# Two-layer hybrid block on one core: triangular substitutions of two groups moved from VectorE to GpSimd, fills re-ordered

## The chip, the cores and the metric

The kernel runs on one core of a Trainium2 chip. The metric is the device time of one execution in microseconds (us), as the median of several runs.

## What is computed

Two layers of a diffusion backbone over 512 latent tokens and 256 context tokens of width 1024. In each layer one projection of the normalised input feeds three token mixers, which are gated, projected and merged:

```python
h = rms_norm(x, norm_g) * (1.0 + scale) + shift
za, ga, zb, gb, zc, gc, zg = jnp.split(h @ w_in, list(IN_CUTS), axis=-1)
ya, yac = rwkv7_branch(za, zac, ...)
yb = dense_block_attention(qb_, jnp.concatenate([kbc, kb_], axis=1), ...)
yc = window_attention(qc_, kc_, vc_, kcc, vcc, c_sink)
x_new = x + gate * merge_branches((ya, yb, yc), (ga, gb, gc), zg, w_branch_out, w_out)
```

The change sits in the first mixer, a recurrence over tokens in both directions, with one 64x64 state S for each of 8 heads:

```python
def step(S, inp):
    r_t, w_t, k_t, v_t, kk_t, a_t = inp
    sa = jnp.einsum('bhvk,bhk->bhv', S, kk_t)
    S = (S * w_t[:, :, None, :] - sa[..., None] * (kk_t * a_t)[:, :, None, :]
         + v_t[..., None] * k_t[:, :, None, :])
    return S, jnp.einsum('bhvk,bhk->bhv', S, r_t)
```

## The kernel before

**The recurrence in chunks.** The 768 tokens are cut into 12 chunks of 64 (`NCH`), and the scan over tokens becomes a scan over chunks. Within a chunk the update needs the inverse of a 64x64 unit triangular matrix for each head and direction. `rwkv_inverse` makes the inverses of a group of four chunks at once (`NS` = 4, `NG` = 3 groups a layer). It loads the matrices (`TT`, four DMAs, L641 and L642), transposes 32x32 blocks on VectorE (L647), cuts out a triangle on GpSimd (`affine_select`, L651), and inverts the 32x32 diagonal blocks by substitution: 30 values of j, each with a multiply (L657) and an add (L659) on VectorE, of j·(31−j) elements per partition, each reading what the one before wrote. Then two transposes on VectorE (L662, L663), and matmuls for the off-diagonal blocks on TensorE: `zp`, then `yp`, in two halves (n0). GpSimd clears a part of the result (L684).

**A chunk's step.** `rwkv_step` is a chain through PE and the engines that empty PSUM: `Rp` (state times input), `Up` (inverse times Rp), `Sp` and `Yp` (new state, output). `rwkv_scores` prepares the products of the chunk two ahead (`scps`, masked on VectorE at L623 and L625). So every `Rp` on PE in the trace is the start of one step. The inverse of the next group is made meanwhile, by a generator `ahead`, which is advanced once behind each of the first three steps of a group; its matmuls come in the group's fourth step (i % NS == NS − 1). The fourth step cannot be passed without them, since `in_line()` keeps PE's instructions in the order in which the code emits them.

**Fills.** Between the pieces of the chain PE works on other projections (`tiles`, `proj`, `gemm_steps`), which have no part in the recurrence. `pace(n)` emits n units of them. In layer 0 a unit is a quarter of the 24 matmuls (12 of 512 columns, 12 of 256) that use one loaded piece of weights; in layer 1 it is 3 matmuls. A piece of weights is loaded as `wf` (L162), copied by ScalarE to a rounded part `wh` (L165), and GpSimd makes the rest `wl` (L166); `wf`, `wh` and `wl` have four buffers each. The table `FILL` gives for each layer: units ahead of the recurrence, units at its first inverse, units at each yield of that inverse's matmuls, units at the three pieces of a step (and of a group's fourth step), units at the last readout. What is left of the fills runs at the end of the layer's attention, with nothing between.

**What sets the order.** A list scheduler orders each engine's instructions by priority bands: `band(b)`, lower first, and SERVE = −1 (weights and what empties PSUM for the fills) ahead of all. With B = 10·layer, scores and steps are in B + 1, the fills of the first inverse in B + 4. Every engine and SyncE's DMA queue then run in that fixed order, each instruction waiting for its inputs and its buffer.

Of the kernel before, what the change touches and what calls it, by code (L numbers as in the profile page):

```python
# [14 lines left out]
ALU = mybir.AluOpType  # L15
# [4 lines left out]
P = 128  # L20
# [9 lines left out]
GB, RB, CB = 2, 3, 2  # L30


FILL = ((48, 36, 2, (2, 2, 2), (3, 3, 3), 2), (72, 56, 4, (2, 2, 2), (3, 3, 3), 2))

QUEUES = (("scalar", "sync", "sync", "scalar"), ("sync", "scalar", "sync", "sync"))

# [1 line left out]
NS, NG = 4, 3  # L38
# [22 lines left out]
def build(tc, A, out):  # L61
    nc = tc.nc
    V, S, G, TE, DMA = nc.vector, nc.scalar, nc.gpsimd, nc.tensor, nc.sync
# [11 lines left out]
    @contextmanager  # L75
    def band(b):

        keep, mine = tc.cur_priority, bands.get(b, b * 1000000)
        tc.cur_priority = mine
        yield  # L80
        bands[b] = tc.cur_priority
        tc.cur_priority = keep
# [64 lines left out]
    @contextmanager  # L147
    def in_line():
        line["on"] = True
        yield  # L150
        line["on"] = False

    def mm(o, l, r, start=True, stop=True, **kw):
        queued(TE.matmul(o, l, r, start=start, stop=stop, **kw))  # L154
# [336 lines left out]
    def rwkv(l, D, last, DL, B, pace, zlast):  # L491

        with tc.tile_pool(name="rw", bufs=1, reuse_waits="tile") as rp:
            yo = rp.tile([P, 4, T], F32, name="yo")
            st = {"seen": set(), "S": None}
            parts, YB = {}, {}

            def scores(i):
                if i < NCH:
                    parts[i] = yield from rwkv_scores(l, last, rp, i)  # L500

            def invert(g):
                if g < NG:
                    YB[g] = rp.tile([P, 32, 64], F32, tag="YB", name="YB", bufs=2)
                    yield from rwkv_inverse(l, rp, g, YB[g])

            def rest(*gens):
                for g in gens:
                    for _ in g:
                        pass  # L510

            with band(B + 1):
                rest(scores(0), scores(1))
                ahead = invert(0)
                for _ in range(3):
                    next(ahead)
            with band(B + 4), tc.issue_after(zlast):
                pace(FILL[l][1])
            with band(B + 1), in_line():
                for _ in ahead:  # L520
                    pace(FILL[l][2])
                ahead = out = iter(())
                for i in range(NCH):
                    if i % NS == 0:
                        rest(ahead)
                        ahead = invert(i // NS + 1)
                    nxt = scores(i + 2)
                    step = rwkv_step(l, last, i, yo, st, DL, rp, parts.pop(i), YB[i // NS])
                    for n in FILL[l][3 if i % NS < NS - 1 else 4]:
                        next(step, None)  # L530
                        next(nxt, None)
                        if i % NS == NS - 1:
                            next(ahead, None)
                        next(out, None)
                        pace(n)
                    rest(step, nxt)
                    if i % NS < NS - 1:
                        next(ahead, None)
                    if i in READY and (i > 3 or not last):
                        rest(out)  # L540
                        out = readout(l, D, rp, yo, READY[i])
                for _ in out:
                    pace(FILL[l][5])

# [90 lines left out]
    def rwkv_inverse(l, rp, g, YB):  # L635

        TT = rp.tile([P, 8, NS, 64], F32, tag="TT", name="TT")
        cs = slice(g * NS, (g + 1) * NS)
        for b0 in (0, 64):

            DMA.dma_start(TT[b0:b0 + 32], tt_d[l][b0:b0 + 32, :, cs])  # L641
            DMA.dma_start(TT[b0 + 32:b0 + 64, :, :, 0:32], tt_d[l][b0 + 32:b0 + 64, :, cs, 32:64])  # L642
        inv = rp.tile([P, 1536], F32, tag="inv", name="inv")
        MB, tmp = inv[:, 0:1024], inv[:, 1024:1536]
        YK = YB[:, :, 32:64]
        TT4 = TT.rearrange("p c s t -> p (c s) t")
        V.transpose(MB, TT4[:, :, 0:32].rearrange("p n j -> p j n"))  # L647

        M3 = MB.rearrange("p (j i) -> p i j", i=32)
        Y3 = YK.rearrange("p j i -> p i j")  # L650
        G.affine_select(YK, MB.rearrange("p (j i) -> p j i", i=32),  # L651
                        [[1, 32], [-1, 32]], ALU.is_gt, 0.0, base=0, channel_multiplier=0)
        V.memset(YB.rearrange("p n c -> p (n c)")[:, 32:2048:65], 1.0)
        for j in range(30, 0, -1):
            n = 31 - j
            t3 = tmp[:, 256 * (j % 2):256 * (j % 2) + j * n].rearrange("p (i c) -> p i c", c=n)
            V.tensor_tensor(t3, M3[:, 0:j, j:j + 1].to_broadcast([P, j, n]),  # L657
                            Y3[:, j:j + 1, j + 1:32].to_broadcast([P, j, n]), ALU.mult)
            V.tensor_tensor(Y3[:, 0:j, j + 1:32], Y3[:, 0:j, j + 1:32], t3, ALU.add)  # L659
            if j in (22, 12):  # L660
                yield
        V.transpose(YB[:, :, 0:32].rearrange("p n j -> p j n"), YK)  # L662
        V.transpose(MB.rearrange("p (n j) -> p n j", j=32), YB[:, :, 0:32])  # L663
        for b0 in (32, 96):
            S.copy(YB[b0:b0 + 32, :, 32:64], YB[b0:b0 + 32, :, 0:32])
        X13 = MB.rearrange("p (n j) -> p n j", j=32)
        yield
        for n0 in range(0, 32, 16):
            zp = rps.tile([P, 16, 32], F32, tag="r", name="zp", bufs=RB)
            for n in range(16):  # L670
                for b0 in (0, 64):
                    mm(zp[b0 + 32:b0 + 64, n, :], TT4[b0:b0 + 32, n0 + n, 32:64], X13[b0:b0 + 32, n0 + n, :])
            z3 = tmp.rearrange("p (n j) -> p n j", j=32)
            for b0 in (32, 96):
                S.copy(z3[b0:b0 + 32], zp[b0:b0 + 32])
            yield
            yp = rps.tile([P, 16, 32], F32, tag="r", name="yp", bufs=RB)
            for n in range(16):
                for b0 in (0, 64):
                    mm(yp[b0:b0 + 32, n, :], z3[b0 + 32:b0 + 64, n, :], YB[b0 + 32:b0 + 64, n0 + n, 32:64])  # L680
            S.copy(YB[0:32, n0:n0 + 16, 32:64], yp[0:32])
            V.tensor_copy(YB[64:96, n0:n0 + 16, 32:64], yp[64:96])
        for b0 in (32, 96):
            G.memset(YB[b0:b0 + 32, :, 0:32], 0.0)  # L684
# [731 lines left out]
    for l in range(2):  # L1416
        last = l == 1
# [3 lines left out]
        B = 10 * l  # L1421
# [22 lines left out]
        def tiles():  # L1444

            zb = [(T_CQ + j, zb_d[l][j], (LAT,) if last and j < 2 else BOTH, "raw") for j in range(4)]
            zc = [(T_ZC + j, zb_d[l][4 + j], (LAT,) if last and j < 4 else BOTH, "raw") for j in range(6)]
            ga, gb, gc = ([(t + j, g_d[l][4 * n + j], segs, "silu") for j in range(4)]
                          for n, t in enumerate((T_GA, T_GB, T_GC)))
            todo = zb[2:] + zc[4:] + zc[:4] + zb[:2] + ga + gb if last else zb + ga + gb + zc  # L1450
            todo += gc + [(T_ZG + j, th_zg[l][j], segs, "tanh") for j in range(24)]
            for a in todo:
                yield from proj(l, hh, hl, *a, side)
                yield

        steps = tiles()

        def pace(n):

            for _ in zip(range(n), steps):  # L1460
                pass
# [3 lines left out]
        with band(B + 4):  # L1465
            pace(FILL[l][0])
        ss = cpool.tile([P, 6, 10], F32, tag="ss", name="ss")
        if last:
            cctx.close()
            with band(B + 3):  # L1470
                gqa_tokens(l, F, last, ss)
        rwkv(l, D, last, DL, B, pace, zlast)
        weights["queue"] = getattr(nc, QUEUES[l][2])
        with band(B + 4), tc.issue_after(line["last"]):
            pace(22 * 8 - sum(FILL[l][0:2]) - 2 * FILL[l][2] - NG * (3 * sum(FILL[l][3]) + sum(FILL[l][4])) - 4 * FILL[l][5])

# [162 lines left out]
```

## Time and profile before

| | |
|---|---|
| median of 3 runs | 2433.22 us (2431.24 to 2439.78) |
| profiled execution, time / span | 2433.78 / 2432.1 us |
| mean granted TensorE clock | 0.947 |
| PE busy | 2166.8 us (89%) |
| DVE (VectorE) busy | 1278.8 us (53%) |
| ACT (ScalarE) busy | 894.1 us (37%) |
| POOL (GpSimd) busy | 844.3 us (35%) |

Shares are averages over stages with different limits. The recurrence of layer 0 runs from about 360 to 660 us of the span, that of layer 1 from about 1690 to 1920 us. A timeline row gives start, duration, engine, line, operation, what it writes and reads, shape and count; in brackets the idle time ahead of it and what ended that.

### The profile page before, as it was taken

Reading aid. Unit: us, or ns where it says so; the run is one execution under the profiler, and the core shown is the slowest. Engines: PE = TensorE matmul, PEld = TensorE weight load, DVE = VectorE, ACT = ScalarE, POOL = GpSimd, SP = SyncE. Lnnn points to the kernel's source line nnn. Section 1 sums busy time; section 2 is a strip of 40 time slices with the busy share of each in tenths; the row PEclk is TensorE's granted clock in tenths of the full one; section 3 lists DMA queues with packets and bytes.
Section 4 is the critical chain, followed back from the end, with each engine's and each line's share of the span. In section 5 each row is a group of like instructions: output and inputs, shape, how many; then the busy total and the mean of one; then the engine's idle time right before and its main releaser. Section 6 shows DMA issues by size and latency. Waiting matters only on the chain. (4 is left out here: it accounts for less than half of the span.)

```text
span 2432.1 us, 42833 instructions
## 1 busy us (share of the span) xinstructions
PE 2166.8 (89%) x16824; PEld 1657.7 (68%) x16824; DVE 1278.8 (53%) x2300; ACT 894.1 (37%) x1654; POOL 844.3 (35%) x699
## 2 busy tenths in 40 slices
PE   7988895888998999899989998798968998999989
PEld 4766683667877666766767786666756876666667
DVE  5466326865347663466145356736577456545223
ACT  4443221223354333543222345332322465334322
POOL 1244221111123444444333224443211144454464
PEclk9998997998999999999999999899988999999989
DMA  7146665445251013511685314665553262011474
GB/s 251 61 137 195 199 198 129 127 127 140 73 176 50 20 53 95 172 36 47 217 269 172 122 61 125 180 194 160 134 124 88 90 208 87 18 52 36 139 248 159
DMA packets 330442, 314.25 MB, mean 129 GB/s; under 512 B 112768, under 2 KB 239488, under 8 KB 330240
## 3 DMA queue, kind: packets, MB, share of 16 engines
q1 hardware_dynamic: 315120, 283.97, 39.2%
q10 hardware_dynamic: 15120, 27.53, 3.5%
q8 instruction: 133, 2.18, 0.4%
q14 instruction: 69, 0.57, 0.1%
HBM read 213.64 MB, written 97.78 MB: 128 GB/s over the span
## 5 line engine op out<-in xcount | busy, mean ns | idle before, releaser
L166 POOL TENSOR_TENSOR wl<-wf,wh 128x512 fp32r<-128x512 f32 x316 | 426.1, 1350 | 1060.1 <-ACT wh L165 979.9
L154 PE MATMUL g<-hh,wh 128*128 128x512 f32 (+1 forms) x1264 | 467.1, 370 | 14.1 <-DVE st L760 11.2
L154 PE MATMUL g<-hh,wl 128*128 128x512 f32 (+1 forms) x1264 | 457.0, 362 | 1.5 <-POOL wl L166 1.5
L154 PE MATMUL g<-hl,wh 128*128 128x512 f32 (+1 forms) x1264 | 454.1, 359 | 0.0
L165 ACT CAST wh<-wf 128x512 fp32r<-128x512 f32 x316 | 195.2, 619 | 503.4 <-PE g L154 233.8
L154 PEld LDWEIGHTS g<-hh,wh 128*128 128x128 f32 x1264 | 247.8, 196 | 66.4 <-issue 14.9
L154 PEld LDWEIGHTS g<-hh,wl 128*128 128x128 f32 x1264 | 247.7, 196 | 43.0 <-issue 9.4
L154 PEld LDWEIGHTS g<-hl,wh 128*128 128x128 f32 x1264 | 248.7, 197 | 38.7 <-issue 10.1
L867 POOL TENSOR_TENSOR acc<-acc,pe 128x512 f32<-128x512 f32 (+2 forms) x128 | 146.3, 1143 | 144.6 <-ACT pe L863 135.0
L863 ACT ACTIVATE pe<-stp 128x256 f32<-128x256 f32 (+2 forms) x224 | 114.5, 521 | 201.7 <-PE stp L154 194.9
L845 DVE TENSOR_REDUCE mx<-mps 128x1 f32<-128x384 f32 (+2 forms) x256 | 127.8, 535 | 68.7 <-PE mps L154 66.4
L154 PE MATMUL yps<-pe,vh 128*64 128x256 f32 (+1 forms) x704 | 132.5, 386 | 0.0
L154 PE MATMUL g<-yh,wh 128*128 128x512 f32 (+1 forms) x224 | 84.8, 384 | 21.9 <-DVE zt L1349 11.0
L1349 DVE SCALAR_TENSOR_TENSOR zt<-zt,g 128x512 f32<-128x512 f32 (+1 forms) x56 | 32.0, 576 | 129.8 <-PE g L154 86.6
L659 DVE TENSOR_TENSOR YB<-YB,inv 128x30 f32<-128x30 f32 (+9 forms) x180 | 91.9, 511 | 5.3
L657 DVE TENSOR_TENSOR inv<-inv,YB 128x30 f32<-128x30 f32 (+9 forms) x180 | 87.8, 488 | 8.9 <-issue 2.8
L154 PE MATMUL g<-yl,wh 128*128 128x512 f32 (+1 forms) x224 | 85.2, 384 | 6.3 <-POOL yl L1334 6.2
L154 PE MATMUL gc<-hh,wh 128*128 128x512 f32 x192 | 79.1, 412 | 7.8 <-ACT hh L325 4.5
L758 ACT ACTIVATE st<-g 128x256 f32<-128x256 f32 (+1 forms) x108 | 56.6, 524 | 76.0 <-PE g L154 66.4
L623 DVE TENSOR_TENSOR AR<-scps,cst 64x256 f32<-64x256 f32 x96 | 40.1, 418 | 82.2 <-PE scps L154 81.1
L154 PE MATMUL g<-yh,wl 128*128 128x512 f32 (+1 forms) x224 | 82.1, 371 | 0.0
L154 PE MATMUL gc<-hl,wh 128*128 128x512 f32 x192 | 79.5, 414 | 0.0
(395 smaller groups left out, 4402.0 us busy)
## 6 DMA issues: line engine op xcount, KB each, us to landing
wf<-w_in SPq DMA_DIRECT2D x159, 256.0 KB, 3.0
wf<-ada_w SPq DMA_DIRECT2D x96, 256.0 KB, 3.7
wf<-w_in ACTq DMA_DIRECT2D x81, 256.0 KB, 3.0
bkd<-bk SPq DMA_DIRECT2D x16, 768.0 KB, 5.2
zt<-thzg SPq DMA_DIRECT2D x48, 256.0 KB, 3.8
wf<-w_bo SPq DMA_DIRECT2D x40, 256.0 KB, 3.3
thzg<-st SPq DMA_DIRECT2D x24, 384.0 KB, 2.3
md<-zt SPq DMA_DIRECT2D x32, 256.0 KB, 3.5
```

The costliest lines, as they stand in the source:

```text
L154: queued(TE.matmul(o, l, r, start=start, stop=stop, **kw))
L165: S.copy(wh, w32)
L166: eng.tensor_tensor(wl, w32, wh.bitcast(F32), ALU.subtract)
L623: V.tensor_tensor(AR[oth, pds, 2 * par, :], ps[oth, :, a0:a0 + 64], msk("ms", oth), ALU.mult)
L657: V.tensor_tensor(t3, M3[:, 0:j, j:j + 1].to_broadcast([P, j, n]), Y3[:, j:j + 1, j + 1:32].to_broadcast([P, j, n]), ALU.mult)
L659: V.tensor_tensor(Y3[:, 0:j, j + 1:32], Y3[:, 0:j, j + 1:32], t3, ALU.add)
L758: S.activation(t[:, sl], p, AF.Tanh, scale=0.5)
L845: V.tensor_reduce(mx, ps, AX.X, ALU.max)
L863: S.activation(e, st, AF.Exp, scale=scale)
L867: G.tensor_tensor(acc, keep.pop(0, acc), e, ALU.add)
L1349: V.scalar_tensor_tensor(th, th, 1.0, p_, ALU.add, ALU.mult)
```

## The change

- The 60 substitution operations of the second and third group of each layer (g > 0) go to GpSimd (`G`); those of the first group stay on VectorE. The transposes and the select stay where they were.
- The whole vector part of the next group's inverse (loads, transpose, select, substitutions, transposes) is emitted at once at the start of a group, in band B + 2, below the steps (B + 1) and below SERVE, where before it came in three pieces behind the first three steps in the steps' own band.
- More units at the first inverse: 64 for 36 in layer 0, 60 for 56 in layer 1.
- In layer 0 the fills' order is zb, zc, ga, gb (was zb, ga, gb, zc). The z tiles are copied out of PSUM by ScalarE alone, the g tiles by ScalarE and then VectorE (L760).

```diff
-FILL = ((48, 36, 2, (2, 2, 2), (3, 3, 3), 2), (72, 56, 4, (2, 2, 2), (3, 3, 3), 2))
+FILL = ((48, 64, 2, (2, 2, 2), (3, 3, 3), 2), (72, 60, 4, (2, 2, 2), (3, 3, 3), 2))
...
                     if i % NS == 0:
                         rest(ahead)
                         ahead = invert(i // NS + 1)
+                        with band(B + 2):
+                            for _ in range(3):
+                                next(ahead, None)
...
                     rest(step, nxt)
-                    if i % NS < NS - 1:
-                        next(ahead, None)
...
+            e = G if g else V
-            V.tensor_tensor(t3, M3[:, 0:j, j:j + 1].to_broadcast([P, j, n]),
+            e.tensor_tensor(t3, M3[:, 0:j, j:j + 1].to_broadcast([P, j, n]),
                             Y3[:, j:j + 1, j + 1:32].to_broadcast([P, j, n]), ALU.mult)
-            V.tensor_tensor(Y3[:, 0:j, j + 1:32], Y3[:, 0:j, j + 1:32], t3, ALU.add)
+            e.tensor_tensor(Y3[:, 0:j, j + 1:32], Y3[:, 0:j, j + 1:32], t3, ALU.add)
...
-            todo = zb[2:] + zc[4:] + zc[:4] + zb[:2] + ga + gb if last else zb + ga + gb + zc
+            todo = (zb[2:] + zc[4:] + zc[:4] + zb[:2] if last else zb + zc) + ga + gb
```

In the changed kernel the lines lie a little lower: L647 is L649, L651 is L653, L657 and L659 are L660 and L662, L662 and L663 are L665 and L666, L623 and L625 are L625 and L627, L641 and L642 are L643 and L644.

GpSimd in layer 0, before, from the select of the first group on to the weights behind the last one (`wl` is the weights' rest):

```order
L651 AFFINE_SELECT YB<-inv 128x32x32
L166 TENSOR_TENSOR wl<-wf,wh 128x512 x2
L684 MEMSET YB 32x32x32 x2
L166 TENSOR_TENSOR wl<-wf,wh 128x512 x2
L651 AFFINE_SELECT YB<-inv 128x32x32
L166 TENSOR_TENSOR wl<-wf,wh 128x512 x3
L684 MEMSET YB 32x32x32 x2
L166 TENSOR_TENSOR wl<-wf,wh 128x512 x2
L651 AFFINE_SELECT YB<-inv 128x32x32
L166 TENSOR_TENSOR wl<-wf,wh 128x512 x6
L684 MEMSET YB 32x32x32 x2
L166 TENSOR_TENSOR wl<-wf,wh 128x512 x18
```

GpSimd in layer 0, changed, at the second group's select and the head of its 60 substitutions:

```order
L687 MEMSET YB 32x32x32 x2
L166 TENSOR_TENSOR wl<-wf,wh 128x512 x10
L653 AFFINE_SELECT YB<-inv 128x32x32
L660 TENSOR_TENSOR inv<-inv,YB 128x30
L662 TENSOR_TENSOR YB<-YB,inv 128x30
L660 TENSOR_TENSOR inv<-inv,YB 128x58
L662 TENSOR_TENSOR YB<-YB,inv 128x29x2
L660 TENSOR_TENSOR inv<-inv,YB 128x84
L662 TENSOR_TENSOR YB<-YB,inv 128x28x3
```

Ten pieces of weights now stand between the first group's end and the second group's select, where two stood; the 60 substitutions follow with no piece of weights among them. The 60 of the third group have one piece in their middle and one behind.

VectorE in layer 0, changed, in the fourth step of the first group, up to the copy of that step's `Up`:

```order
L763 SCALAR_TENSOR_TENSOR st<-st,g 128x512
L625 TENSOR_TENSOR AR<-scps,cst 64x4x64
L627 TENSOR_TENSOR TR<-scps,cst 128x4x64
L625 TENSOR_TENSOR AR<-scps,cst 64x4x64
L627 TENSOR_TENSOR TR<-scps,cst 128x4x64
L649 STREAM_TRANSPOSE inv<-TT 128x1024
L655 MEMSET YB 128x32
L665 STREAM_TRANSPOSE YB<-YB 128x32x32
L666 STREAM_TRANSPOSE inv<-YB 128x1024
L712 COPY UV<-Up 64x512
```

Before, the transpose L647 of this group stood in the first step and L662 and L663 at the end of the third; now the whole chain stands in the fourth step, ahead of the copy of `Up`.

SyncE's queue in layer 0, changed, where the loads of the second group's `TT` end:

```order
L162 DMA wf<-w_in 128x512
L600 DMA AR<-ard_124 64x8x64
L604 DMA UV<-vd_128 64x512
L605 DMA UV<-vd_128 64x512
L594 DMA BK<-bkd_126 64x1024
L596 DMA BK<-bkd_126 64x8x64 x2
L643 DMA TT<-ttd_130 32x8x256
L644 DMA TT<-ttd_130 32x32x32
```

The last two loads of `TT` stand behind a load of weights and six loads of the scores; before, they stood in front of that load of weights.

## Rows read from the trace of the kernel before

**Rows 1.** Busy time by engine in 20 us of fills after layer 0's attention.

```profile
core 0: us, PE busy (x) PEld busy (x) DVE busy (x) ACT busy (x) POOL busy (x), PEclk, DMA share, GB/s
1140.00:1160.00 20.00, 20.00 (x155) 14.27 (x154) 12.63 (x13) 6.95 (x17) 9.54 (x10) 1.00 0.15 40
```

**Rows 2.** Timeline of PE: first inverse of layer 0, and spacing of fills.

```profile
410.29 1.92 PE L154 MATMUL zp<-inv,TT 32*32 32x32 f32 x64 [29.73 <-DVE inv L663]
...
620.98 0.39 PE L154 MATMUL g<-hh,wl 128*128 128x512 f32 x1
621.21 0.28 PE L154 MATMUL g<-hh,wh 128*128 128x256 f32 x1
```

**Rows 3.** Timeline of PE, steps of layer 0: the 1st, 5th, 8th to 10th.

```profile
421.82 1.15 PE L154 MATMUL Rp<-UV,AR 128*64 128x64 f32 x32
...
490.42 1.20 PE L154 MATMUL zp<-inv,TT 32*32 32x32 f32 x64
...
513.98 1.15 PE L154 MATMUL Rp<-UV,AR 128*64 128x64 f32 x32
...
590.16 1.15 PE L154 MATMUL Rp<-UV,AR 128*64 128x64 f32 x32
...
613.42 1.15 PE L154 MATMUL Rp<-UV,AR 128*64 128x64 f32 x32
...
628.63 1.15 PE L154 MATMUL Rp<-UV,AR 128*64 128x64 f32 x32
```

**Rows 4.** Timeline of PE, steps of layer 1: the 1st, 2nd, 5th, 9th, 10th.

```profile
1731.00 1.15 PE L154 MATMUL Rp<-UV,AR 128*64 128x64 f32 x32
...
1741.71 1.15 PE L154 MATMUL Rp<-UV,AR 128*64 128x64 f32 x32
...
1790.54 1.92 PE L154 MATMUL zp<-inv,TT 32*32 32x32 f32 x64 [13.83 <-DVE inv L663]
...
1809.84 1.15 PE L154 MATMUL Rp<-UV,AR 128*64 128x64 f32 x32
...
1889.28 1.15 PE L154 MATMUL Rp<-UV,AR 128*64 128x64 f32 x32
...
1902.28 1.15 PE L154 MATMUL Rp<-UV,AR 128*64 128x64 f32 x32
```

**Rows 5.** Costliest groups (busy us, mean ns | idle before): adds of the substitution.

```profile
L659 DVE TENSOR_TENSOR YB<-YB,inv 128x30 f32<-128x30 f32 (+9 forms) x180 | 91.9, 511 | 5.3
```

**Rows 6.** Timeline of DVE: an add that overlapped a `wl` on POOL.

```profile
381.98 1.49 DVE L659 TENSOR_TENSOR YB<-YB,inv 128x168 f32<-128x168 f32 x1
```

**Rows 7.** Timeline of POOL: multiplies of 256 and 128 contiguous elements.

```profile
962.32 0.74 POOL L1122 TENSOR_TENSOR ccq<-rtc,fp 128x256 f32<-128x256 f32 x1 [4.25 <-DMA raw<-zbd]
963.01 0.87 POOL L1126 TENSOR_TENSOR scq<-rtc,fp 128x128 f32<-128x128 f32 x2
```

**Rows 8.** One line that runs on both engines (duration ns min/median/max).

```profile
L1030 POOL TENSOR_TENSOR kt<-krt,ss x6: 659/1059/1327, 762.9 to 2034.1; 128x256 f32<-128x256 f32 x6
L1030 DVE TENSOR_TENSOR kt<-krt,ss x6: 409/622/1481, 763.5 to 2041.1; 128x256 f32<-128x256 f32 x6
```

**Rows 9.** Timelines of POOL and DVE: select and transposes of one inverse.

```profile
374.69 1.27 POOL L651 TENSOR_SCALAR_AFFINE_SELECT YB<-inv 128x1024 f32<-128x1024 f32 x1 [3.28 <-DVE inv L647]
...
407.07 1.89 DVE L662 STREAM_TRANSPOSE YB<-YB 128x1024 f32<-128x1024 f32 x1
408.99 1.25 DVE L663 STREAM_TRANSPOSE inv<-YB 128x1024 f32<-128x1024 f32 x1
```

**Rows 10.** Timeline of SyncE's queue: issue of a load of `TT`.

```profile
505.45 0.61 SPq L642 DMA_DIRECT2D TT<-ttd  x1
```

**Rows 11.** DMA issues: count, KB each, us from issue to landing.

```profile
TT<-ttd SPq DMA_DIRECT2D x12, 256.0 KB, 4.4
```

**Rows 12.** Timeline of DVE in free steps of layer 0 and layer 1.

```profile
619.87 0.69 DVE L709 COPY UV<-Up 64x512 f32<-64x512 f32 x1 [2.65 <-ACT UV L708]
...
621.70 0.41 DVE L625 TENSOR_TENSOR TR<-scps,cst 128x256 f32<-128x256 f32 x1
...
1899.45 0.43 DVE L695 COPY UV<-So 64x512 f32<-64x512 f32 x1
```

## The prediction

> **What bounds the kernel now.** I read the busy time by stretches first. Where only fills run, TensorE (PE) is busy for all of 20.00 us [rows 1]: a fill taken out of there shortens the span by its own length. The timeline of PE then shows where PE stands still. The largest single gap is at the first inverse of layer 0: 29.73 us in front of `zp`, ended by the last transpose on VectorE (DVE) [rows 2]. The steps come next. The start of each `Rp` marks a step: free ones take 628.63 − 613.42 = 15.2 us in layer 0 [rows 3] and, in layer 1, 1741.71 − 1731.00 = 10.7 us (without output) or 1902.28 − 1889.28 = 13.0 us (with it) [rows 4]. While an inverse is made beside them they take longer: the four steps of the second group of layer 0 take 613.42 − 513.98 = 99.4 us [rows 3], where three free steps and a fourth with the matmuls of an inverse (613.42 − 590.16 = 23.3) would take 3 x 15.2 + 23.3 = 68.9. The difference is DVE's substitutions, which push masks and copies of the chain back. So the change goes for real time. The question is what comes in its place.
>
> **How long the substitutions take now.** A group's 60 operations have j(31 − j) elements each, 165 on average. On DVE an add takes 511 ns [rows 5], so 60 take about 30 us. Call S the time of the 60 on GpSimd (POOL). No row shows them there. From below: contiguous multiplies of 256 elements start 963.01 − 962.32 = 0.69 us apart, and two of 128 take 0.87, 0.435 each [rows 7]; at 165 elements that lies at 0.435 + 37/128 x 0.26 = 0.51, S = 31. Each operation here reads what the one before wrote, so none starts early; with the 0.05 us by which the two rows overlap (0.74 against 0.69), S = 34. From above: one line runs on both engines, with a broadcast operand as here, and POOL's median is 1059 against DVE's 622 ns, 1.70 times as long [rows 8]; 1.70 x 30 gives S = 51. The substitutions jump through memory by rows and broadcast, so they are nearer to the second: I take 0.75 us each, **S = 45**, and keep 31 and 51 for the range.
>
> The page "GPSIMD Engine Reference" of the Trainium skill (section "Engine selection") speaks against the change: elementwise work with two inputs is to stay on VectorE, since GpSimd takes about twice as long. The rows agree in direction (1.70). By that rule S would be 60, an estimate, and the sum below would be +126 instead of +66.
>
> **Fills at the first inverse, layer 0.** 28 units more, 6 matmuls each; a matmul of 512 columns holds PE for 621.21 − 620.98 = 0.23 us [rows 2], one of 256 half of that, so a unit is 6 x 0.175 = 1.05 us and 28 are 29.4 us: as much as the gap of 29.73. They come out of the fills after attention, which are full [rows 1], so the gain is their length. Against that: seven more pieces of weights go through POOL during DVE's substitutions, and an add that overlapped one took 1.49 us [rows 6] where the mean is 0.511 [rows 5]; 7 x 0.98 = 6.9 us that `zp` comes later. Sum: **−22.5** (bounds −29.4 and −15, with twice the delay). That the z tiles come before the g tiles costs nothing: both are the same matmuls, and ScalarE, which empties both, idles there. The four units more in layer 1 have no such gap to fill: 0.
>
> **Second group, layer 0.** By the order, POOL has the select and the substitutions behind ten pieces of weights, in one run. The last of these needs a buffer that PE frees only at the end of the third step, because a piece holds one of four buffers until its matmuls are done. Behind it on SyncE's queue stand a load of weights, six of scores and two of `TT`, eight at 0.61 us [rows 10] = 4.9, then 4.4 to land [rows 11]. Then DVE's transpose (1.9), select (1.3), S, two transposes (1.9 + 1.25) [rows 9]. `zp` of this group stands in the fourth step and cannot be passed. So: 3 x 15.2 + 4.9 + 4.4 + 1.9 + 1.3 + S + 3.1 = 61.2 + S from the first `Rp` to `zp`. Before it was 490.42 − 421.82 = 68.6 [rows 3]. Change: **S − 7.4**. The three steps themselves do run free; what they gain is lost at `zp`.
>
> **Third group, layer 0.** DVE's first transpose stands behind the second masks of the fifth step, 621.70 + 0.41 − 613.42 = 8.7 us into a step [rows 3, 12]; with transpose and select the substitutions start at 11.9. The next transpose stands in DVE's order right behind the copy of `Up` in the step after, 15.2 + (619.87 + 0.69 − 613.42) = 22.3 [rows 12]. DVE waits there, and with it all masks and state updates queued behind, for 11.9 + S − 22.3 = S − 10.4. The four steps take 68.9 + S − 10.4, against 99.4: **S − 40.9**.
>
> **Second group, layer 1.** Three steps of 10.7; the transpose stands behind the first masks of the fourth step, two batches of matmuls (1.15 each [rows 4]) and 1.6 of masks, 3.9 later; then 1.9 + 1.3 + S, with four adds of the rotary embedding among the substitutions (3.3 us, scaled from [rows 7]), and 3.1. `zp` at 45.6 + S; before 1790.54 − 1731.00 = 59.5 [rows 4]. **S − 13.9**.
>
> **Third group, layer 1.** Free: 3 x 13.0 and 13.0 + 8.1 for the inverse (23.3 − 15.2, as in layer 0) = 60.1. The transpose stands behind the last state copy of a step, 1899.45 + 0.43 − 1889.28 = 10.6 [rows 4, 12], so the substitutions start at 13.8; the next transpose is wanted at 13.0 + 10.6 = 23.6. Stall S − 9.8; before the four took 1889.28 − 1809.84 = 79.4 [rows 4]. **S − 29.1**.
>
> **Sum.** 4S − 113.8. With S = 45: **+66 us** on the profiled execution of 2433.78, that is **2500 us** (the median of the three runs is 0.6 us lower, which is nothing here). With S = 31 it is +10 (2444), with S = 51 +90 (2524). It turns at S = 28.5, 0.475 us an operation.
>
> What hides what: weights for the fills wait behind the substitutions on POOL, but PE stands at `zp` meanwhile and needs none; if it did not stand, four buffers last for some 16 units, 17 us, less than S, and PE would run out of weights instead. So there is no way for POOL's 4S = 180 us to cost nothing by the fills' side alone.
>
> **Rivals.**
> 1. *The substitutions are short enough (faster).* If POOL does these small operations in under 0.475 us, the free steps outweigh the stalls, at one place above all: the third groups, where the terms are S − 40.9 and S − 29.1. For it: DVE's substitutions do cost the steps 30 us in layer 0 (99.4 − 68.9). Against: contiguous operations of 128 elements take 0.435 already [rows 7] and the mean here is 165. With S = 22 the sum is −26: 2408 us. Chance 0.15, which also takes in that part of a chain starts earlier than I read from the order.
> 2. *A wash.* S between 27 and 30, or a stall that is smaller by as much: 2434 us, chance 0.07.
> 3. *POOL is twice as slow as DVE.* S = 60, from twice the 30 us of DVE [rows 5]; +126, 2560 us. For it: single executions of the line in [rows 8] reach 1327 ns on POOL, over twice DVE's median. Against: the medians. Chance 0.10. This is also where the rule named above would lead; another section of that page ("Performance pitfalls for Q7 kernels") puts half as much again on strided reads, an estimate of S = 46 from the contiguous rows, which is the forecast's own case.
>
> **How the numbers follow.** The forecast, S between 31 and 55, has 0.68; rival 3 has 0.10, and both are slower: 0.78. The measurement can tell about 0.3%, 7.3 us, from no change. Faster 0.15, same 0.07. The range: from 2440 (S = 30, the lower bound with a little less delay at the first inverse) to 2540 (S = 55, where each operation takes 0.92 us); outside lie most of rival 1 and rival 3, some 0.2.
>
> **What would show it.** Right: in the first inverse of layer 0 the wait at `zp` falls from 29.73 us to a few; the first three steps of each layer's first group take about 15 and 11 us; POOL shows 60 substitutions in a row of about 45 us; `zp` of the second group waits some 55 us in both layers (106 against 48 us from the first `Rp` in layer 0, 91 against 34 in layer 1), ended by DVE's transpose, which itself waited for POOL; in the sixth step of each layer PE stands for 30 us or more, with DVE waiting at the transpose behind a copy. The busy time after attention falls by 29 us in layer 0. Wrong: if `zp` of the second groups waits under 20 us, S is under 28 or the chain began earlier; if the third groups' steps run through, the transpose on DVE did not block; if steps without an inverse take longer than before, POOL's substitutions hold DVE up, which I put at nothing beyond the 45.

## The result and the profile after

The change is slower: 2524.2 us median (2515.81 to 2525.87, 4 runs) against 2434.3 us (4 runs); the ratio is 1.0371, 95% interval 1.0347 to 1.0395. The prediction was 2500 (2440 to 2540), slower with a chance of 0.78. The profiled execution has a span of 2524.1 us and a mean granted clock of 0.930 (0.947 before).

Busy time by engine, and the substitutions among the costliest groups (busy us, mean ns | idle time before):

```profile
PE 2164.1 (86%) x16824; PEld 1650.7 (65%) x16824; DVE 1168.2 (46%) x2060; ACT 894.4 (35%) x1654; POOL 982.2 (39%) x939
...
L662 POOL TENSOR_TENSOR YB<-YB,inv 128x30 f32<-128x30 f32 (+14 forms) x120 | 75.9, 632 | 9.3
```

PE has as much work as before (2164.1 us busy against 2166.8), so the 92 us of span are idle time of PE. The starts of `Rp` in PE's timeline show where, as the rows of [rows 3, 4] did before:

```profile
442.05 1.15 PE L154 MATMUL Rp<-UV,AR 128*64 128x64 f32 x32
...
547.81 1.92 PE L154 MATMUL zp<-inv,TT 32*32 32x32 f32 x64 [56.13 <-ACT YB L668]
...
572.34 1.15 PE L154 MATMUL Rp<-UV,AR 128*64 128x64 f32 x32
...
629.97 1.97 PE L154 MATMUL Yp<-AR,So 64*64 64x64 f32 x32 [26.74 <-DVE TR L627]
...
680.27 1.15 PE L154 MATMUL Rp<-UV,AR 128*64 128x64 f32 x32
...
1771.55 1.15 PE L154 MATMUL Rp<-UV,AR 128*64 128x64 f32 x32
...
1866.29 1.91 PE L154 MATMUL zp<-inv,TT 32*32 32x32 f32 x64 [13.75 <-DVE inv L666]
...
1886.65 1.15 PE L154 MATMUL Rp<-UV,AR 128*64 128x64 f32 x32
...
1978.26 1.15 PE L154 MATMUL Rp<-UV,AR 128*64 128x64 f32 x32
```

The differences of such rows give the table of stages that all that follows uses. "Between" runs from layer 0's ninth `Rp` to layer 1's first, "rest" from layer 1's ninth to the end. `before_again` is the kernel before, profiled once more beside later runs; between its two profiles the long stretches "between" and "rest" differ by 5.4 and 2.5 us.

| us | first Rp | L0 steps 1-4 | 5-8 | between | L1 steps 1-4 | 5-8 | rest |
|---|---|---|---|---|---|---|---|
| before | 421.8 | 92.2 | 99.4 | 1117.6 | 78.8 | 79.4 | 542.8 |
| before_again | 422.3 | 92.5 | 99.4 | 1112.2 | 79.7 | 77.8 | 540.3 |
| the change | 442.1 | 130.3 | 107.9 | 1091.3 | 115.1 | 91.6 | 545.8 |
| fills_only | 439.8 | 93.3 | 94.5 | 1089.2 | 79.0 | 78.2 | 555.0 |
| fills_48 | 432.2 | 89.8 | 97.5 | 1108.5 | 80.3 | 77.6 | 541.1 |
| todo_only | 421.1 | 92.4 | 99.4 | 1111.0 | 78.8 | 79.4 | 544.2 |
| after_on_dve | 439.6 | 117.7 | 93.4 | 1090.8 | 106.0 | 83.3 | 553.3 |
| after_no_subs | 443.6 | 93.6 | 91.1 | 1090.0 | 75.0 | 64.0 | 549.8 |
| after_old_place | 441.2 | 104.1 | 112.6 | 1095.8 | 88.4 | 91.0 | 553.3 |
| after_late | 449.5 | 117.9 | 117.6 | 1092.0 | 107.6 | 88.8 | 548.9 |
| after_late_swap | 444.6 | 118.0 | 93.8 | 1093.6 | 108.5 | 74.4 | 552.9 |
| swap | 420.8 | 103.2 | 116.2 | 1110.0 | 86.2 | 91.7 | 544.4 |
| swap_late | 418.1 | 78.3 | 93.0 | 1123.0 | 70.2 | 71.6 | 546.9 |
| swap_late_48 | 429.3 | 85.3 | 89.7 | 1112.1 | 71.0 | 72.1 | 546.8 |

The change lost 38.1 + 8.5 us in layer 0's first eight steps and 36.3 + 12.2 in layer 1's, 95 us together. What happens in the first of these, from the timelines of POOL and DVE in the change:

```profile
503.13 1.27 POOL L653 TENSOR_SCALAR_AFFINE_SELECT YB<-inv 128x1024 f32<-128x1024 f32 x1 [12.83 <-DVE inv L649]
504.48 0.24 POOL L660 TENSOR_TENSOR inv<-inv,YB 128x30 f32<-128x30 f32 x1
...
523.53 0.83 POOL L662 TENSOR_TENSOR YB<-YB,inv 128x240 f32<-128x240 f32 x1
524.43 0.72 POOL L660 TENSOR_TENSOR inv<-inv,YB 128x240 f32<-128x240 f32 x1
...
544.25 0.26 POOL L662 TENSOR_TENSOR YB<-YB,inv 128x30 f32<-128x30 f32 x1
```

```profile
544.54 1.89 DVE L665 STREAM_TRANSPOSE YB<-YB 128x1024 f32<-128x1024 f32 x1 [39.96 <-POOL YB L662]
...
627.04 1.89 DVE L665 STREAM_TRANSPOSE YB<-YB 128x1024 f32<-128x1024 f32 x1 [27.33 <-POOL YB L662]
```

POOL starts in the fourth step and needs 544.51 − 504.48 = 40.0 us, 0.67 us an operation: S = 40. DVE stands in front of its transpose for all of it, and PE at `zp`. In the third group (second row of the second fence) DVE stands for 27.3 us. In layer 1's second group PE's wait is in five pieces, 13.9, 4.9, 8.9 and 13.8 us ahead of small matmuls between 1807 and 1852 us and the 13.75 at `zp`: 55.3 together.

### The profile page after: what moved, and what is told of

It is laid out like the page before. It is cut to its first block, busy times and chain, and to the rows that moved or that the text cites. A ratio compares the mean times of both kernels' runs of the same rounds, so it can differ in the third digit from the quotient of the medians.

```text
span 2524.1 us, 42817 instructions
## 1 busy us (share of the span) xinstructions
PE 2164.1 (86%) x16824; PEld 1650.7 (65%) x16824; DVE 1168.2 (46%) x2060; ACT 894.4 (35%) x1654; POOL 982.2 (39%) x939
## 5 line engine op out<-in xcount | busy, mean ns | idle before, releaser
L154 PE MATMUL g<-hh,wh 128*128 128x512 f32 (+1 forms) x1264 | 469.6, 372 | 17.4 <-DVE st L763 12.6
L154 PEld LDWEIGHTS g<-hl,wh 128*128 128x128 f32 x1264 | 249.9, 198 | 41.0 <-issue 12.2
L625 DVE TENSOR_TENSOR AR<-scps,cst 64x256 f32<-64x256 f32 x96 | 40.1, 417 | 111.4 <-PE scps L154 110.5
L662 POOL TENSOR_TENSOR YB<-YB,inv 128x30 f32<-128x30 f32 (+14 forms) x120 | 75.9, 632 | 9.3
L870 POOL TENSOR_TENSOR acc<-pe 128x512 f32<-128x512 f32 (+1 forms) x48 | 52.6, 1096 | 65.2 <-ACT pe L866 64.2
L154 PE MATMUL gc<-hh,wl 128*128 128x512 f32 x192 | 77.6, 404 | 0.0
```

What stands on the lines that cost most here:

```text
L625: V.tensor_tensor(AR[oth, pds, 2 * par, :], ps[oth, :, a0:a0 + 64], msk("ms", oth), ALU.mult)
L662: e.tensor_tensor(Y3[:, 0:j, j + 1:32], Y3[:, 0:j, j + 1:32], t3, ALU.add)
L870: G.tensor_tensor(acc, keep.pop(0, acc), e, ALU.add)
```

## Experiments

**1. The engine and the place, in the change.** Three kernels: the substitutions back on VectorE, nearly all of them left out, and the old place with GpSimd.

```diff
# after_on_dve
-            e = G if g else V
+            e = V
# after_no_subs
+            if g and j not in (30, 22, 12):
+                continue
# after_old_place
-                        with band(B + 2):
-                            for _ in range(3):
-                                next(ahead, None)
...
+                    if i % NS < NS - 1:
+                        next(ahead, None)
```

`after_on_dve`. Expected:

> The change as it is, but all substitutions back on VectorE (the late place and the fills stay). Theory (four stalls, each as long as the substitutions S, from a start that the order fixes): S falls from 40 to some 31 us, so 4 x 9 = 36 us less: about 2488 us. Rival 'place': where the chain stands costs, not the engine; 2515 to 2525. Rival 'engine': GpSimd is the whole loss (its port, its weights held up); about 2433.

Measured: 2488.2 us, ratio to before 1.0251 (1.0222 to 1.0279). That is the theory's 2488, though in part by luck: the second group's substitutions in layer 0 take 530.27 − 501.71 = 28.6 us here, from the first to the transpose behind the last, where the theory reckoned with 31, and four times the full difference would be 46 us. The change's medians differ by 36 us, by the ratios it is 29. In the late place a third of the loss goes with the engine; the rest stays with VectorE.

`after_no_subs`. Expected:

> The change, but of the 60 substitutions of the second and third group only 6 are done (j = 30, 22, 12); the rest of that computation is left out. Theory: S falls from 40 to about 4. The second groups' stalls (56 us and 55 us against the free arrival) shrink by the full 36, the third groups' (27 and 28 us) vanish: 36 + 36 + 27 + 27 = 126 us less, about 2398. Rival 'place': the late loads and transposes make most of the stall; at most 40 us less, 2484 or more. Rival 'clock and fills': the loss sits in the first inverse and the clock; under 30 us less.

Measured: 2405.2 us, 0.9903 (0.9874 to 0.9931). The theory again, within 7 us of its 2398 (119 us less by the medians, 114 by the ratios, where 126 were forecast): the substitutions' duration is on the path in all four groups, which get shorter by 36.7, 16.8, 40.1 and 27.6 us. In layer 0's third group, where 27 were forecast, PE then waits for other things, a load of `AR` (6.7 us) and a copy on ScalarE (3.9 us) above all.

`after_old_place`. Expected:

> The change, but the inverse is advanced as before, one piece behind each of the first three steps, in the steps' band; substitutions of groups 2 and 3 stay on GpSimd, fills as changed. Theory: the select now comes in the first step (14 us after the first Rp), S is about 46 with five pieces of weights among it, so zp comes at 14 + 2 + 1.3 + 46 + 3 = 66 us against 106 in layer 0, and by 20 to 30 us earlier in layer 1; the third groups gain 10 to 20 each: 2430 to 2450. Rival 'engine': GpSimd's time is paid wherever the chain stands; 2500 or more. Rival 'better on GpSimd': the steps are free of substitutions and the fills gain; under 2420.

Measured: 2480.0 us, 1.0210 (1.0180 to 1.0240). This is neither the theory's time nor the rival's: the early start gave 44 us back by the medians (39 by the ratios), at least 30 less than the theory said. With `fills_only` (below: VectorE, old place) these make a square of four kernels with equal fills: old place 1.0024 on VectorE and 1.0210 on GpSimd, late place 1.0251 and 1.0371. So each of the two edits alone costs about 2% and both together 3.5%. One reason why GpSimd may cost in the old place too stands in SyncE's queue (us in total, times, longest), for `after_old_place` and then for the kernel before over the same eight steps:

```profile
SPq L162 <- POOL wl L166: 89.4, 12, 28.3
```

```profile
SPq L162 <- POOL wl L166: 22.8, 7, 10.1
```

A load of weights waits for a buffer that a `wl` on POOL frees; the `wl` stands behind substitutions; and behind the load, in the same queue, stand the loads of the next chunk. PE's `scps` then waits for a DMA (12.9 us at 497.8 us of the span). As a theory, these were the missing 30 us and more; the next kernels try it. The same trace shows a second wait that the theory left out: DVE stands for 56.7 us in front of the two transposes of these eight steps, 29.0 at most, until POOL's substitutions end.

**2. GpSimd and VectorE swapped.** From the kernel before: substitutions of the later groups to GpSimd in the old place, and `wl` of the fills inside the steps to VectorE. Then the same with the transposes behind the substitutions held in VectorE's order.

```diff
# swap
-        eng.tensor_tensor(wl, w32, wh.bitcast(F32), ALU.subtract)
+        weights.get("eng", eng).tensor_tensor(wl, w32, wh.bitcast(F32), ALU.subtract)
...
+                weights["eng"] = V
...
+            e = G if g else V
# swap_late, besides
+        if g:
+            yield
-        V.transpose(YB[:, :, 0:32].rearrange("p n j -> p j n"), YK)
+        first = V.transpose(YB[:, :, 0:32].rearrange("p n j -> p j n"), YK)
+        if g:
+            tc.add_manual_dep(first.ins, line["dve"].name, ...)
...
-        V.tensor_copy(UV[OD, 1, :, :], Up[OD])
+        line["dve"] = V.tensor_copy(UV[OD, 1, :, :], Up[OD]).ins
```

`add_manual_dep` puts the transpose behind the copy of `Up` on the same engine, with no semaphore; the loop is changed so that the inverse's last matmuls may come between `Rp` and `Up` of the next group's first step.

`swap`. Expected:

> The kernel before, with the substitutions of groups 2 and 3 on GpSimd in the old place (one piece behind each of the first three steps), and in return the weights' rest wl of the fills inside the recurrence's steps on VectorE; fills as before. Theory 'queue': in the old place GpSimd's substitutions cost because wl waits behind them, a weight load on SyncE's queue waits for wl, and the loads of the chunks stand behind that; with wl on VectorE the 46 us vanish and the steps lose the 30 us of DVE's substitutions in part: second groups about 10 us shorter than before, third groups about 15, each in two layers, less what wl costs on VectorE: 2385 to 2415. Rival 'engine': GpSimd's 40 us a group are on the path in any case, 2470 or more. Rival 'port': VectorE and GpSimd slow each other down, no gain, 2425 to 2450.

Measured: 2481.7 us, 1.0208 (1.0185 to 1.0231). The theory failed by 67 us or more, and the time lies where the rival 'engine' had put it (2470 or more). Freeing the queue alone gave nothing (1.0208 against 1.0210 in `after_old_place`). The trace of `swap` shows what the theory had left out. PE's wait, DVE's timeline, and DVE's waits in total:

```profile
483.74 1.97 PE L154 MATMUL Up<-Rs,YB 64*64 64x64 f32 x32 [24.87 <-ACT Rs L705]
```

```profile
479.04 1.89 DVE L665 STREAM_TRANSPOSE YB<-YB 128x1024 f32<-128x1024 f32 x1 [26.86 <-POOL YB L662]
```

```profile
DVE YB L665 <- POOL YB L662: 53.2, 2, 26.9
```

SyncE's queue waited only 18.7 us for `wl` over 420 to 640 us of the span (9.8 at most), and POOL began at 437.50, in the second step, and had ended at 479.0. But the fixed order has DVE's transpose as early as the third step (its `Rp` is at 453.7), where, it seems, the scheduler reckons POOL to be done; masks, copies and state updates stand behind it.

`swap_late`. Expected:

> The kernel 'swap' with the same hold: substitutions of groups 2 and 3 on GpSimd from the first step of the group on, wl on VectorE, transposes behind the copy of Up in the fourth step. Theory: swap lost its gain to VectorE standing at the transpose for 27 to 31 us in each of the four groups; three of these go, of the one in layer 1's second group 8 us: steps 1 to 4 and 5 to 8 take about 72 and 85 us in layer 0 (103 and 116 in swap, 92 and 99 before), 78 and 65 in layer 1 (86 and 92; 79 and 79): 2480 - 90 = 2390, below both kernels. Rival 'engine': GpSimd's 41 us stay on the path wherever they stand: 2460 or more. Rival 'something else is late next': 2400 to 2460.

Measured: 2399.2 us, 0.9879 (0.9860 to 0.9898): below both kernels, by 30 us below the one before. So the rival 'engine' is out: with the same substitutions on GpSimd the kernel is faster than with VectorE's, once the transposes are held. Ahead of these transposes DVE stood for 112.9 us over the whole span in the change, for 111.6 in `swap` and for 29.5 here. Whether `wl` had to move as well is not shown in the old place, since no kernel there had the hold alone. Its timeline of PE:

```profile
418.05 1.15 PE L154 MATMUL Rp<-UV,AR 128*64 128x64 f32 x32
...
485.69 1.38 PE L154 MATMUL zp<-inv,TT 32*32 32x32 f32 x64 [1.90 <-DVE yo L751]
...
496.39 1.15 PE L154 MATMUL Rp<-UV,AR 128*64 128x64 f32 x32
...
1774.91 1.92 PE L154 MATMUL zp<-inv,TT 32*32 32x32 f32 x64 [18.66 <-DVE inv L675]
```

In layer 0 `zp` waits 1.9 us, where the change has 56.1, though the substitutions run on the same engine for as long (434.69 to 477.66, 43 us). Three waits of PE are left, of which the theory, with its 2390, had reckoned with the first alone: 18.7 us at `zp` of layer 1's second group, whose first three steps (10.7 to 11.5 us each) are too short to hide S behind; 10.0 us just ahead of `zp` in layer 1's third group, for masks behind the held transpose; and 11.3 us in layer 0's seventh step, for a load of `AR`.

**3. The same two waits in the change itself.** `after_late` holds the transposes; `after_late_swap` also moves `wl` to VectorE. The edits are those of `swap_late`, made to the change.

`after_late`. Expected:

> The change, with one thing moved: for groups 2 and 3 the transposes behind the substitutions are held, in VectorE's order, behind the copy of Up of the group's fourth step, and the inverse's matmuls may end as late as the Up of the step after. Theory (VectorE stands at the transpose, which the fixed order puts ahead of what GpSimd can deliver): the third groups' stalls of 27 and 28 us in layer 0 and 1 shrink to some 2 and 12, the second groups stay as they are, since their whole chain starts late: about 40 us less than the change, 2475 to 2495. Rival 'the engine costs in any order': no more than 10 us less, 2510 to 2525.

Measured: 2516.2 us, 1.0350 (1.0326 to 1.0375); the theory asked for 40 us and got 8 by the medians, 5 by the ratios. The first `Rp` came 7.4 us later than in the change, of which 4.6 us were there before the first inverse; the cause was not found. In layer 0's third group the wait moved, and in layer 1 as well. PE in layer 0, SyncE's queue there, and ScalarE in layer 1:

```profile
641.51 1.83 PE L154 MATMUL scps<-AR,BK 64*128 64x128 f32 x13 [33.88 <-DMA UV<-vd]
```

```profile
SPq L162 <- POOL wl L166: 112.3, 8, 49.7
```

```profile
ACT UV L705 <- POOL wl L166: 18.1, 1, 18.1
ACT UV L719 <- POOL wl L166: 12.5, 1, 12.5
```

With DVE free, PE stands 33.9 us for a chunk's load, in a queue that waited up to 49.7 us for a `wl`. In layer 1 the weights are loaded from ScalarE's queue, and it is ScalarE's own copies in the chain (`UV`) that come 18.1 and 12.5 us late.

`after_late_swap`. Expected:

> The change with the transposes held (as in after_late) and wl of the steps' fills on VectorE (as in swap). Theory (two waits behind the substitutions, either of which alone keeps the third groups' stall: VectorE at the transpose, and the queue that issues weight loads, SyncE's in layer 0 and ScalarE's in layer 1, at a load that waits for wl): with both gone the third groups come to the times of swap_late, 93 us in layer 0 (118 in after_late) and 72 in layer 1 (89), 42 us less than after_late; the second groups still start late: 2455 to 2480. Rival 'place and order are all': the third groups do not change, 2505 to 2520. Rival 'the late start was the queue too': the second groups come to swap_late's 78 and 70 us as well, 2400 to 2415.

Measured: 2484.1 us, 1.0224 (1.0205 to 1.0242); 32 of the 42 us, 4 us above the range that the theory gave. The third groups come to 93.8 and 74.4 us, those of `swap_late`; the second groups stay at 118 and 108.5. So what is left of the loss, some 55 us, stands in the second groups (25.8 and 29.7 us more than before), which start late; `swap_late` differs from this kernel by the place and the fills, and there they take 78.3 and 70.2. Either wait alone keeps the third groups' stall: the transpose alone in `swap` (old place, 116.2 and 91.7), the queue alone in `after_late` (late place, 117.6 and 88.8).

**4. The fills.** Three kernels from the one before: all of the fills' edits; the new order with 48 units and layer 1 as before; the order alone. And one from `swap_late`.

```diff
# fills_only
-FILL = ((48, 36, ...), (72, 56, ...))
+FILL = ((48, 64, ...), (72, 60, ...))
-            ... else zb + ga + gb + zc
+            ... else zb + zc + ga + gb
# fills_48, swap_late_48: the order, and
-FILL = ((48, 36, ...
+FILL = ((48, 48, ...
# todo_only: the order alone
```

`fills_only`. Expected:

> The kernel before with the new FILL and the new order of the fills alone. As forecast, the first inverse of layer 0 gains 22 us: 2411. As the trace of the change reads (first Rp of layer 0 20 us later, the stretch behind the recurrence 26 us shorter): 6 us less, 2427. Rival: nothing or a loss, since zp stands behind fills that end 13 us after the inverse is there; 2434 to 2445.

Measured: 2434.1 us, 1.0024 (1.0010 to 1.0038): the rival, a small loss.

`fills_48`. Expected:

> The kernel before with the new order of the fills and 48 units at the first inverse of layer 0 (36 before, 64 in the change); layer 1 as before. Theory: in the change 28 units took 51 us from the end of the old fills to zp, 1.8 us each, and the inverse was there after 37, so 20 fit; 12 fit with room, gain 12 x 1.05 less 4 us by which wl delays the substitutions on VectorE: 8 us less, 2422 against 2430. Rival: what the gap gains is given back later, as with 64: within 3 us of before.

Measured: 2428.9 us, 0.9993 (0.9980 to 1.0006): no difference, the rival again.

`todo_only`. Expected:

> The kernel before with the new order of the fills alone (z tiles before g tiles in layer 0), 36 and 56 units as before. As forecast: nothing, within 3 us of before. Rival: fewer VectorE operations among the first inverse's substitutions (the g tiles' silu), 3 to 5 us less; rival: the z tiles of the attention are there sooner or the g tiles later where they are wanted, a difference of either sign over 4 us.

Measured: 2430.9 us, 1.0003 (0.9988 to 1.0017): nothing, as forecast.

`swap_late_48`. Expected:

> swap_late with the new order of the fills and 48 units at the first inverse of layer 0. Theory (fills moved into the gap give back what they gain, as 48 and 64 did in the kernel before): within 4 us of swap_late, 2395 to 2403. Rival 'the gap is worth it where the steps no longer lose it': 8 to 12 us less, 2387 to 2391.

Measured: 2409.9 us, 0.9930 (0.9912 to 0.9947). Slower than `swap_late` by 0.5%, where 4 us were allowed: in its profile the first `Rp` comes 11.2 us later, of which the stretch "between" gives back 10.9, and the four steps behind it lose 7.0. Why these four steps are longer was not looked into.

`before_again`, the unchanged kernel in one execution (2426.0 us), gave the second row of the table:

> The kernel before, unchanged, for a profile from the same chip as the runs beside it: every stage within 1% of the first profile by all theories.

Layer 0's stages agree within 1%, layer 1's to 0.9 and 1.6 us (1.1 and 2%), a little more than was expected; the wait at the first inverse is the same (29.6 against 29.7 us).

Why the gap of 29.7 us did not pay: in the change, by windows of 10 us (the columns of [rows 1]), from where it began:

```profile
380.00:390.00 10.00, 9.12 (x48) 7.11 (x52) 8.86 (x17) 2.11 (x4) 2.69 (x2) 0.83 0.47 157
390.00:400.00 10.00, 8.83 (x51) 5.91 (x44) 9.55 (x16) 2.12 (x4) 2.29 (x2) 1.00 0.76 198
400.00:410.00 10.00, 7.74 (x36) 4.94 (x36) 9.55 (x21) 0.07 (x1) 0.60 (x1) 0.69 0.37 118
410.00:420.00 10.00, 9.46 (x58) 7.46 (x61) 8.41 (x16) 4.18 (x6) 3.98 (x4) 0.97 0.48 133
```

PE issues 36 to 58 matmuls in 10 us there, stands idle for 4.9 of the 40 us, and the granted clock falls to 0.69 in one window. From 375.9 us up to `zp` it runs 188 matmuls of fills and 64 of the conditioning (`modps`), which ride along with each piece of weights; before, from the same place to `zp`, 20 and 8. So the 28 units are 168 matmuls, and they brought 56 of 256 columns with them, some 7 us that ran beside the steps before. And the fills end late. The inverse's last transpose, from DVE's timeline, and PE's `zp`:

```profile
416.85 1.25 DVE L666 STREAM_TRANSPOSE inv<-YB 128x1024 f32<-128x1024 f32 x1
```

```profile
431.51 1.20 PE L154 MATMUL zp<-inv,TT 32*32 32x32 f32 x64
```

From the end of the transpose (418.1) `zp` is held up for 13.4 us by fills that stand ahead of it.

## Why the prediction was right, and where it was not

**The mechanism and the sign: right.** Four stalls that grow with S about one for one, each from a start that the order fixes. `after_on_dve` and `after_no_subs` measure that: 36 us by the medians for S from 40.0 to 28.6 (the rule of four would say 46; the four stages give 12.6, 14.5, 9.1 and 8.3, together 44), 119 us for leaving nine tenths of the substitutions out. These two show the sum's form, 4S less a constant. That the number came out so near is in part luck: at the measured S the prediction's sum would be +46 us, half of what was measured, and S put too long made up for 20 of the 46 us that the other terms had too little.

**S: 45 put, 40.0 measured.** The nearest row should have been the contiguous one [rows 7], not the line that runs on both engines [rows 8]: an operation of 240 elements took 0.83 us and one of 30 took 0.26. The Trainium skill's rule (page "GPSIMD Engine Reference", section "Engine selection": about twice as long as VectorE for two inputs) would have given 60, an estimate; here it is 40.0 against 28.6 us in `after_on_dve`, 1.4 times as long.

**Second group, layer 0 (S − 7.4): 32.6 with the measured S, 38.1 in the trace.** Right in kind: `zp` waits 56.1 us; 55 were named. The number agrees by luck: the substitutions began 504.48 − 442.05 = 62.4 us behind the first `Rp`, where 58.1 were put, and S was 5 us shorter.

**Third group, layer 0 (S − 40.9): −0.9 with the measured S, +8.5 in the trace.** DVE's stall was 27.3 us, where S − 10.4 = 29.6 was put. What failed is the free step of 15.2: the fifth and seventh steps took 591.20 − 572.34 = 18.9 and 656.63 − 637.63 = 19.0. In the fifth PE also runs ten matmuls of the readout (`pr`), was busy for 17.6 us against 15.2 in a free step, and idle for 1.2. In the seventh it runs the matmuls of a free step, but behind the long idle time of the sixth: it stood 1.9 us for loads of `AR`, and the granted clock was 0.91 over the step, 1.00 in a free one. And the prediction saw one wait there; `after_late` shows a second behind it, the queue of weight loads.

**Second group, layer 1 (S − 13.9): 26.1 with the measured S, 36.3 in the trace.** The first transpose came 1816.51 − 1805.17 = 11.3 us into the fourth step, not 3.9, since the last load of `TT` was issued only at 1811.27 and lands some 4.4 us later [rows 11]. The load's place in SyncE's queue was counted in layer 0 and not here.

**Third group, layer 1 (S − 29.1): 10.9 with the measured S, 12.2 in the trace.** Right within 1.3 us, though DVE stood for 33.9 us at the transpose, where S − 9.8 = 30.2 was put.

**Fills (−22.5): the term that failed.** The stretch behind the recurrence did become 26.3 us shorter (29.4 put), and the inverse came later by 414.78 − 407.07 = 7.7 us (6.9 put). But the first `Rp` came 20.2 us later, not 6.9, because a unit in the gap took (431.5 − 380.6)/28 = 1.8 us and not 1.05 (380.6 is where PE's wait of [rows 2] began), so the fills outlasted the inverse. `fills_only` puts the whole term at 0.24% to the bad. The last column of the table, too, is 549 to 555 us in the six other kernels with 60 units in layer 1 (546 in the change) and 540 to 547 in those with 56; no kernel changed that number alone, so this part stays open.

**"There is no way for POOL's 4S = 180 us to cost nothing by the fills' side alone": too strong for the idea, though it was said of a kernel with `wl` on POOL.** In `swap_late`, with `wl` on VectorE, all four groups run on POOL, and at three of the four PE waits under 2 us at `zp`. Whether it holds while `wl` stays on POOL is not shown: no kernel had `wl` there together with the early start and the hold.

**Sum.** S was 5 too long (20 us), the four places 26.4 us too cheap at the measured S, the fills 16.4 us too good, and the rest 3 us longer: 66.2 − 20 + 26.4 + 16.4 + 3 = 92.

## What to carry to other kernels

Work that moves to another engine takes its place in that engine's queue, and every in-order queue that waits for something behind it moves too: here the engine's other products, the DMA queue that needs their buffers, and the loads behind that. The consumer has a place in a fixed order as well, and if the producer is slower than the scheduler reckons, the consumer's engine stands still for all that is behind; hold the consumer back by hand, and look for a second wait under the first before the idea is given up. A gap is worth filling only with as much as fits at the rate that work has in the gap, not at its rate in a full stretch.

## What was not expected of the hardware

GpSimd's substitutions with strides and broadcasts took 0.72 and 0.83 us for 240 elements, next to 0.74 for 256 contiguous ones [rows 7], that is 3.0 and 3.5 ns an element against 2.9: the access pattern cost little. After an idle stretch PE is slow for a while: the granted clock was 0.50 (1.2 of 2.4 GHz) from 500 to 550 us, in which PE was busy for 2.2 us, 0.80 in the next 10 us and 1.00 after that, and the `zp` that ended the wait took 1.92 us against 1.20.

```profile
500.00:550.00 50.00, 2.19 (x65) 2.16 (x66) 5.12 (x4) 2.32 (x3) 38.55 (x63) 0.50 0.00 0
550.00:560.00 10.00, 9.77 (x193) 8.23 (x193) 2.89 (x6) 2.83 (x6) 1.27 (x1) 0.80 0.09 28
560.00:580.00 20.00, 19.42 (x324) 16.26 (x322) 6.78 (x14) 7.37 (x14) 2.55 (x2) 1.00 0.51 114
```
